# Two output projection tiles per layer as one seven-product block multiplication

## The chip, the core and the metric

The kernel runs on one core of a Trainium2 chip, in one launch. The metric is the device time of a run in microseconds; lower is better. The engines are TensorE (PE: matrix products; PEld: its weight loads), VectorE (DVE), ScalarE (ACT), GpSimd (POOL) and SyncE (SP), which issues most DMA transfers. Each engine takes its own queue in order; a wait at the head of a queue holds all that stands behind it.

## The reference

Two layers of a hybrid decoder on 512 tokens and 16 learned meta tokens in front, width 1024, all in fp32:

```python
for l in range(DEPTH):                       # DEPTH = 2
    h = rmsnorm(h_res, norm_gain[l])
    proj = h @ w_in[l]
    u_pool, z_pool, c_q, c_kv, k_rope, z_mla, g_pool, g_mla = jnp.split(proj, IN_SPLIT_POINTS, axis=-1)
    y_pool = (pool_mix(u_pool, pool_w_group[l], pool_scale[l]) * silu(z_pool)) @ pool_w_up[l]
    o_mla = mla(c_q, c_kv, k_rope, pos, ...)          # 8 heads, latent queries and keys, causal
    y_mla = (o_mla * silu(z_mla)) @ mla_w_up[l]
    merged = sigmoid(g_pool) * y_pool + sigmoid(g_mla) * y_mla
    h_res = h_res + merged @ w_out[l]                 # 1024 x 1024
return h_res[:, N_META:]
```

The change is in the last product, `merged @ w_out[l]`.

## The kernel before

**Layout.** Activations lie transposed: channels on the 128 partitions, tokens along the free axis, eight tiles of 128 channels for the width of 1024. Layer 0 works on all 528 tokens, as two segments of 264 (`FULL`); layer 1 needs only the 512 real tokens after its keys and does them as one segment of 512 (`XTOK`), but its last output tile as two of 256.

**Matrix products.** fp32 accuracy is made from three passes: each operand is split into a high part and a low part, and `mm3` issues high x high, high x low, low x high into the same PSUM bank (lines 181, 182, 183). One chunk of weights is 128 x 512 fp32 (256 KB), four blocks of 128 x 128. SyncE loads it (`raw`, L114), ScalarE copies the high part (`whi`, L176), VectorE subtracts to get the low part (`wlo`, L177). [...]

**The order.** `plan` lists the products in the order of the kernel (`register`), and the generator `stream` runs through the weight chunks of the whole plan, keeps several loaded ahead, and yields after every few matmuls. `go` is the rest of the layer: it pulls `stream` along with `upto(name)`, `fill_now(ns)` (go on for so many nanoseconds of modelled matmul time) and puts element-wise work between; `after(ns, fn)` calls a function after so much modelled time. The engines' final queues are then written by a list scheduler that works through the whole program with its own cost model, and may move an instruction of an engine ahead of others.

**The stages around the change.** The last products of a layer are `mu0` to `mu7` (up-projection of attention, 512 deep, one weight chunk each) and `o0` to `o7` (output projection, 1024 deep, two chunks each). What `ev_mu` does for each mu tile and segment: VectorE multiplies with the gate out of PSUM (L980), GpSimd adds the pooling branch `am[m]` (L982), and `split` makes the high part on ScalarE (L275) and the low part on VectorE (L276); the results `mg[0..7]` (`hh`, `hl`) are the operand of all o tiles. Each o tile is 8 blocks x 3 passes: 24 matmuls per segment. `ev_o` reads the residual (from `xT`, in layer 1 from `scr`), adds 0.5 times the product on VectorE (L996; the halved factor belongs to the sigmoid), stores to `scr` or, in layer 1, to the output `yT`, and in layer 0 has the next layer's sum of squares begun (`square_x`). After `o7` of layer 0 the kernel splits the next layer's input (`split_h`).

**Other places that the change touches.** In the query phase `qr0`, `qr1`, `qn0` to `qn3` run (weights `wqb`), with the statistics in `stat` after `qr1`; attention follows, where GpSimd multiplies at L743 and L832/L834. `tmp()` and `sqt()` hand out scratch tiles, `slot(tag)` tiles with names that are shared over the layer, `mmt()` and `sct()` PSUM banks.

Of the kernel before, what the change touches and what calls it, by code (L numbers as in the profile page):

```python
# [55 lines left out]
SPL = 240  # L56
RET = 12500.0
WARM = 8


def cut(v, bits):
# [10 lines left out]
def trunk(ctx, tc, xT, xrow, mrow, pos, win, wkr, wqb, wkb, wvb, wgr, wpu, wmu, wout, gains, const, yT):  # L72
# [89 lines left out]
    class Gemm:  # L162
        def __init__(self, name, src, width, evac=None, xs=None, segs=None, body=None):
            self.name, self.src, self.width, self.alloc = name, src, width, mmt
            self.evac, self.xs, self.segs, self.body = evac, xs, segs, body
            self.spare = False

    loads = [0]

    def wload(src, n, spare):  # L170
        raw = early.pop(0) if early else fetch(src, n, rawt(), sp)
        loads[0] += 1
        pool, th, tl, nb = (tp, "th", "tl", 2) if loads[0] <= 2 or spare else (wp, "whi", "wlo", 3)
        hi = pool.tile([P, W if pool is tp else 512], F32R, tag=th, name=nm("whi"), bufs=nb)
        lo = pool.tile([P, W if pool is tp else 512], F32R, tag=tl, name=nm("wlo"), bufs=nb)
        act.activation(hi[:, :n], raw[:, :n], AF.Copy)  # L176
        dve.tensor_sub(lo[:, :n], raw[:, :n], hi[:, :n].bitcast(F32))  # L177
        return hi, lo

    def mm3(out, wh, wl, xh, xl, start, stop):  # L180
        first = pe.matmul(out, wh, xh, start=start, stop=False)  # L181
# [8 lines left out]
    def stream():  # L190
        flat = [(g_, c) for g_ in plan for c in range(0, g_.width, 512)]
        names = [g_.name for g_, c in flat]
        for i in (1, names.index((0, "o0")) + 1):
            flat[i], flat[i + 1] = flat[i + 1], flat[i]

        def load(i):
            g_, c = flat[i]
            n = min(512, g_.width - c)
# [118 lines left out]
    class Layer:  # L317
        def __init__(self, l):
            self.l, self.last = l, l == DEPTH - 1
            self.XS = XTOK if self.last else FULL  # L320
            self.x0 = NM if self.last else 0
            self.xt = xt if l == 0 else [None] * 8
            self.hs, self.us, self.zps = hbuf, [None] * 4, [None] * 4
            self.cs, self.cqs, self.ys, self.am = [None] * 2, [None] * 6, [None] * 4, [None] * 8
            self.kn, self.qn, self.zms, self.ogs = [None] * 4, [None] * 4, [None] * 4, [None] * 4
            self.qr, self.qf = [None] * 2, [None] * 2
            self.gms, self.mg, self.xr, self.vw = [None] * 8, [None] * 8, [None] * 8, []
            self.made = [None] * 8
            self.csq, self.xsq = [None] * 2, [None] * 8
            self.sq = []  # L330
            self.hosted = self.st = self.acc = self.inv = self.cinv = self.kraw = self.kp = None

        def g(self, c):
            return gn[:, self.l * N_GAIN + c:self.l * N_GAIN + c + 1]
# [640 lines left out]
        def ev_mu(self, m):  # L975
            def ev(ps, a, b):
                if a == self.x0:
                    self.mg[m] = self.hs[m]
                t = tmp()
                dve.scalar_tensor_tensor(out=t[:, :b - a], in0=self.gms[m][:, a:b], scalar=1.0, in1=ps,  # L980
                                         op0=ALU.add, op1=ALU.mult)
                gp.tensor_add(t[:, :b - a], t[:, :b - a], self.am[m][:, a:b])  # L982
                split(*self.mg[m], t[:, :b - a], a, b)
            return ev

        def ev_o(self, m, nxt):
            def ev(ps, a, b):
# [19 lines left out]
        def register(self, nxt):  # L1007
            l, XS = self.l, self.XS
            wi = lambda t: win[l, t]
            hs, ys, cs = (lambda: self.hs), (lambda: self.ys), (lambda: self.cs)  # L1010

            def add(name, src, width, **kw):
                plan.append(Gemm((l, name), src, width, **kw))

            for m in range(2):
                if (l, m) == (0, 1):
                    plan[-1].alloc = sct
                add(f"ckv{m}", wi(MT_CKV + m), D, evac=self.ev_ckv(m), xs=hs, segs=FULL)
# [24 lines left out]
            y(2)  # L1043
            cq(5)
            y(3)
            for r in range(2):
                add(f"qr{r}", wqb[l, r], 768, evac=self.ev_qr(r), xs=lambda: self.cqs, segs=XS)
            for p in range(4):
                add(f"qn{p}", wqb[l, 2 + p], 768, evac=self.ev_qn(p), xs=lambda: self.cqs, segs=XS)
            for m in range(8):  # L1050
                add(f"pu{m}", wpu[l, m], 512, evac=self.ev_pu(m), xs=ys, segs=XS)
            for m in range(4):
                add(f"zm{m}", wi(MT_ZM + m), D, evac=self.ev_silu(self.zms, "u", m), xs=hs, segs=XS)
            for m in range(8):
                add(f"gp{m}", wi(MT_GP + m), D, evac=self.ev_gp(m), xs=hs, segs=XS)
            for m in range(8):
                add(f"gm{m}", wi(MT_GM + m), D, evac=self.ev_gm(m), xs=hs, segs=XS)
            for m in range(8):
                add(f"mu{m}", wmu[l, m], 512, evac=self.ev_mu(m), xs=lambda: self.ogs, segs=XS)
                plan[-1].spare = m % 2 == 1  # L1060
                if (l, m) in ((0, 2), (0, 5)):
                    plan[-1].alloc = sct
            mg = lambda: self.mg
            for m in range(8):
                add(f"o{m}", wout[l, m], D, evac=self.ev_o(m, nxt), xs=mg,
                    segs=[(NM, NM + SEQ // 2), (NM + SEQ // 2, T)] if self.last and m == 7 else XS)
                if (l, m) == (0, 1):
                    plan[-1].alloc = sct

        def gap(self):  # L1070
            fill(FILL[self.l], (self.l, RESERVE[self.l]))

        def go(self, nxt):
# [143 lines left out]
```

## Time and profile before

| | |
|---|---|
| median of 3 runs | 770.41 us (770.23 to 770.59) |
| profiled execution, span from first to last instruction | 768.5 us |
| PE busy | 763.8 us, 99% of the span |
| DVE busy | 544.1 us, 71% |
| ACT busy | 408.9 us, 53% |
| POOL busy | 201.6 us, 26% |
| HBM read, written | 76.69 MB, 4.29 MB |

The only time that the profile gives for its execution is the span; it leaves out what lies ahead of the first and behind the last instruction, and is 1.9 us below the median. Busy time is the time in which an engine had an instruction running; a row of the timeline has start and duration in us, the engine, the line of the kernel, and out<-in. A row's count x2 or x3 means neighbours of the same kind drawn together. "Idle ... <-" names what ended the idle time ahead of it. A row of the windows has, for each engine, busy time and in brackets the instructions, then the granted TensorE clock (1.00 is full speed), the share of the DMA engines and GB/s.

### The profile page before, as it was taken

To read this page: it belongs to the slowest core of one execution; us is meant where nothing else is said; L and a number is where in the kernel's file an instruction comes from. 1 tells how busy PE (TensorE), PEld (TensorE's weight loads), DVE (VectorE), ACT (ScalarE), POOL (GpSimd) and SP (SyncE) were. 2 spreads that over 40 slices of the span, in tenths; PEclk is the share of its full clock that TensorE was granted. 3 is DMA by queue.
4 is the path that set the end of the run, shared out by engine and by line. 5 is a ranking of instruction groups with operands and counts; after the bars stand their busy time and mean duration, and the time that the engine had idled before them with its cause. 6 is when DMAs were issued, how large, how long until landed. Compare 5 with 4: busy or idle time off the path is not lost.

```text
span 768.5 us, 14355 instructions
## 1 busy us (share of the span) xinstructions
PE 763.8 (99%) x5195; PEld 697.9 (91%) x5195; DVE 544.1 (71%) x1179; ACT 408.9 (53%) x892; POOL 201.6 (26%) x251
## 2 busy tenths in 40 slices
PE   9999999999999999999999999999999999999998
PEld 9999999999999999999997898887888888888887
DVE  5588687357899977785376486773677989775842
ACT  6755656545556665634264355454446666664320
POOL 2026204012242233052220262040132434420500
PEclk9999999999999999999999999999999999999999
DMA  8533233343223222325642333334433332222372
GB/s 293 160 113 98 75 97 98 104 141 105 89 79 91 84 71 70 107 71 169 178 133 97 110 86 89 96 87 127 125 119 90 94 93 77 82 69 70 119 222 98
DMA packets 54931, 84.05 MB, mean 109 GB/s; under 512 B 10006, under 2 KB 18582, under 8 KB 54860
## 3 DMA queue, kind: packets, MB, share of 16 engines
q1 hardware_dynamic: 54716, 82.87, 35.6%
q8 instruction: 41, 0.67, 0.4%
q14 instruction: 30, 0.25, 0.1%
q10 hardware_dynamic: 144, 0.26, 0.1%
HBM read 76.69 MB, written 4.29 MB: 105 GB/s over the span
## 4 chain that ended last, share of the span: by engine, by line
PE 99%; DMA 0%; ACT 0%; DVE 0%; SPq 0%; issue 0%; ACTq 0%
PE mm L181 29%; PE mm L183 29%; PE mm L182 29%; PE mm L859 2%; PE S L181 2%; PE S L182 2%; PE S L183 2%; PE o L876 1%; PE o L872 1%; PE S L503 1%; PE S L470 0%; DMA xb<-xT 0%; PE S L806 0%; PE mm L922 0%; PE mm L395 0%; PE S L872 0%
## 5 line engine op out<-in xcount | busy, mean ns | idle before, releaser
L181 PE MATMUL mm<-hh,whi 128*128 128x264 f32 (+2 forms) x1080 | 339.9, 317 | 0.0
L182 PE MATMUL mm<-hl,whi 128*128 128x264 f32 (+2 forms) x1080 | 338.2, 314 | 0.0
L183 PE MATMUL mm<-hh,wlo 128*128 128x264 f32 (+2 forms) x1080 | 337.1, 315 | 0.0
L177 DVE TENSOR_TENSOR wlo<-raw,whi 128x512 fp32r<-128x512 f32 (+2 forms) x251 | 186.7, 748 | 98.6 <-ACT whi L176 94.6
L176 ACT ACTIVATE whi<-raw 128x512 fp32r<-128x512 f32 (+2 forms) x251 | 150.2, 602 | 181.3 <-PE mm L182 135.3
L181 PEld LDWEIGHTS mm<-hh,whi 128*128 128x128 f32 x1080 | 202.5, 188 | 12.9 <-ACT kp L474 0.4
L182 PEld LDWEIGHTS mm<-hl,whi 128*128 128x128 f32 x1080 | 203.0, 188 | 12.2
L183 PEld LDWEIGHTS mm<-hh,wlo 128*128 128x128 f32 x1080 | 201.9, 188 | 12.2
L743 POOL TENSOR_TENSOR tmp<-kp,bc 64x528 f32<-64x528 f32 x16 | 25.6, 1600 | 123.9 <-PE mm L183 70.0
L604 POOL TENSOR_TENSOR racc<-racc,tmp 128x264 f32<-128x264 f32 (+1 forms) x15 | 14.3, 956 | 133.1 <-ACT tmp L603 133.1
L832 POOL TENSOR_TENSOR pm<-pa,rs 128x16 f32<-128x16 f32 x32 | 9.1, 285 | 126.1 <-DVE rs L827 126.1
L982 POOL TENSOR_TENSOR tmp<-tmp,xb 128x264 f32<-128x264 f32 (+1 forms) x24 | 26.9, 1138 | 56.0 <-DVE tmp L980 55.9
L774 DVE CUSTOM_DVE_ANT_0 S<-S,maskw,nqs 128x400 f32<-128x400 f32 (+4 forms) x80 | 38.4, 499 | 4.4 <-PE S L183 4.0
L781 ACT ACTIVATE cq<-S,bia 128x400 f32<-128x400 f32 (+2 forms) x48 | 24.6, 516 | 27.1 <-DVE bia L774 18.1
L181 PE MATMUL mm<-u,whi 128*128 128x264 f32 (+1 forms) x108 | 34.7, 322 | 0.0
L181 PE MATMUL mm<-cq,whi 128*128 128x264 f32 (+1 forms) x108 | 34.7, 321 | 0.0
L183 PE MATMUL mm<-u,wlo 128*128 128x264 f32 (+1 forms) x108 | 34.7, 321 | 0.0
L183 PE MATMUL mm<-cq,wlo 128*128 128x264 f32 (+1 forms) x108 | 34.5, 321 | 0.0
L182 PE MATMUL mm<-cq,whi 128*128 128x264 f32 (+1 forms) x108 | 34.5, 321 | 0.0
L834 POOL TENSOR_TENSOR cq<-cq,rs 128x384 f32<-128x384 f32 (+1 forms) x32 | 32.8, 1024 | 0.0
L276 DVE TENSOR_TENSOR tl<-mm,th 128x384 fp32r<-128x384 f32 (+1 forms) x48 | 27.9, 596 | 5.0 <-ACT th L275 4.8
L275 ACT ACTIVATE th<-mm 128x384 fp32r<-128x384 f32 (+1 forms) x48 | 24.1, 523 | 10.2 <-PE mm L859 9.2
(270 smaller groups left out, 1378.6 us busy)
## 6 DMA issues: line engine op xcount, KB each, us to landing
raw<-win SPq DMA_DIRECT2D x143, 256.0 KB, 2.6
raw<-wout SPq DMA_DIRECT2D x32, 256.0 KB, 3.0
bc<-kdr SPq DMA_DIRECT2D x16, 264.0 KB, 3.6
raw<-wpu SPq DMA_DIRECT2D x16, 256.0 KB, 2.7
raw<-wmu SPq DMA_DIRECT2D x16, 256.0 KB, 2.7
raw<-wqb SPq DMA_DIRECT2D x12, 256.0 KB, 2.6
xb<-xT SPq DMA_DIRECT2D x8, 264.0 KB, 5.7
tmp<-xT SPq DMA_DIRECT2D x16, 132.0 KB, 3.4
```

Of the source, the lines that this page charges most:

```text
L176: act.activation(hi[:, :n], raw[:, :n], AF.Copy)
L177: dve.tensor_sub(lo[:, :n], raw[:, :n], hi[:, :n].bitcast(F32))
L181: first = pe.matmul(out, wh, xh, start=start, stop=False)
L182: pe.matmul(out, wh, xl, start=False, stop=False)
L183: newest[0] = pe.matmul(out, wl, xh, start=False, stop=stop)
L275: act.activation(hi[:, a:b], src, AF.Copy)
L276: return dve.tensor_sub(lo[:, a:b], src, hi[:, a:b].bitcast(F32))
L743: gp.tensor_mul(kf[r0:r0 + 64, :], self.kp[r0:r0 + 64, :], bc[r0:r0 + 64, :])]
L774: return dve.tensor_tensor_reduce(out=sv, in0=sv, in1=mask, scale=nqs[:, i, h:h + 1], scalar=3e38, op0=ALU.add, op1=ALU.min, accum_out=bia ...
L781: act.activation(pv, sv, AF.Exp, scale=-1.0, bias=bia[:, i:i + 1], accum_out=rs[:, c:c + 1])
L834: gp.tensor_mul(pt[i][:, NM:], pt[i][:, NM:], rs[:, i:i + 1].to_broadcast([P, n - NM]))
L982: gp.tensor_add(t[:, :b - a], t[:, :b - a], self.am[m][:, a:b])
```

## The change

Tiles `o6` and `o7` of each layer become one block product. With the merged activations X (1024 deep: upper half 0 to 3, lower half 4 to 7; tokens in two halves) and the two 1024 x 128 weight tiles, the 2 x 2 block product is made from seven products of sums (Strassen's scheme in a variant with shared sums) instead of eight: per product 4 blocks x 3 passes = 12 matmuls of 264 columns (layer 0) or 256 (layer 1).

- `weight_sums`, called after the statistics that follow `qr1`: four sums of weight blocks, formed in DRAM. SyncE issues four copies from `wout` to new DRAM tiles, GpSimd four DMAs that add to them (`accum_op=ALU.add`), with `fill_now(2 * LAG)` between. `pair_operand` gives `stream` the seven chunks: three plain, four sums. All seven are split into high and low as before; that is seven chunks instead of four.
- `combine`: sums of activation quarters on VectorE, 16 per layer; `combine_split`: their high part on ScalarE (L1023 of the new kernel) and low part on VectorE (L1024), 16 each per layer. The first sums start from `ev_mu` with a lag, the others and the splits between `up("mu7")` and `up("o7")` with `fill_now(PACE)` ahead of each.
- `ev_mu`: the pooling sum is written into `am[m]` in place (the sums need it in fp32), and the split reads it there.
- `pair_body`: the seven products use three PSUM banks; a bank is added up over several products (`start=False`), and VectorE adds the bank with 0.5 or -0.5 to the residual after each (L1069), seven times instead of four (layer 0) or three (layer 1). The residual is loaded as one whole tile per m. The built queue has the products of layer 1 in the order 0, 1, 3, 2, 5, 4, 6.

The core of the diff:

```diff
+PAIRS = (3,)
+PACE = 1000.0
...
             def ev(ps, a, b):
...
-                gp.tensor_add(t[:, :b - a], t[:, :b - a], self.am[m][:, a:b])
-                split(*self.mg[m], t[:, :b - a], a, b)
+                f = self.am[m][:, a:b]
+                gp.tensor_add(f, t[:, :b - a], f)
+                split(*self.mg[m], f, a, b)
+                if b == T:
+                    after(LAG, lambda: self.combine(1 if m < 4 else 3, m % 4))
...
+        def combine(self, w, k):
...
+            if w == 1:
+                eng.tensor_sub(f, lo[:, a0:b0], lo[:, a1:b1])
+            elif w == 2:
+                eng.tensor_add(f, hi[:, a1:b1], self.tf[1, k])
+            elif w == 3:
+                eng.tensor_sub(f, hi[:, a1:b1], lo[:, a1:b1])
+            else:
+                eng.tensor_sub(f, self.tf[2, k], hi[:, a0:b0])
+
+        def combine_split(self, w, k):
+            if w in (2, 4):
+                self.combine(w, k)
...
+            act.activation(th, f, AF.Copy, scale=sign)
+            dve.scalar_tensor_tensor(out=tl, in0=f, scalar=sign, in1=th.bitcast(F32), op0=ALU.mult, op1=ALU.subtract)
+
+        def weight_sums(self):
+            acc = lambda d, src: behind(gp.dma_start(d, src, accum_op=ALU.add, max_dma_last_dim=2048), newest[0])
...
+                for d, src in ((s1, w(1, 0)), (s3, w(1, 0)), (s2, w(0, 0)), (s4, w(0, 1))):
+                    behind(sp.dma_start(d, src), newest[0])
+                fill_now(2 * LAG)
+                acc(s1, w(1, 1))
+                acc(s3, w(0, 0))
+                fill_now(2 * LAG)
+                acc(s2, s1)
+                fill_now(2 * LAG)
+                acc(s4, s2)
+
+        def pair_operand(self, p):
...
+                return wload((raw(0, 0), raw(0, 1), s2, s1, s3, s4, raw(1, 1))[i], 512, i % 2 == 1)
...
+            def product(ps, w, xs, start):
+                for k in range(4):
+                    wh, wl = (x[:, k * P:(k + 1) * P] for x in w)
+                    xh, xl = xs[k]
+                    for j, (u, v) in enumerate(((wh, xh), (wh, xl), (wl, xh))):
+                        newest[0] = pe.matmul(ps, u, v, start=start and k == 0 and j == 0, stop=k == 3 and j == 2,
+                                              skip_group_check=not start)
...
+                if i == 0:
+                    product(B, w, quarter(0, a0, b0), True)
+                    add(m1, a0, b0, B, 0.5, False)
+                elif i == 1:
+                    product(A, w, quarter(4, a0, b0), True)
+                    add(m1, a0, b0, A, 0.5, True)
+                elif i == 2:
+                    product(B, w, ts(2), False)
+                    add(m1, a1, b1, B, 0.5, False)
+                elif i == 3:
+                    product(C, w, ts(1), True)
+                    add(m2, a1, b1, C, -0.5, False)
+                elif i == 4:
+                    product(B, w, ts(3), False)
+                    add(m2, a1, b1, B, -0.5, True)
+                elif i == 5:
+                    product(C, w, quarter(4, a1, b1), False)
+                    add(m1, a1, b1, C, 0.5, True)
+                else:
+                    product(B, w, ts(4), False)
+                    add(m2, a0, b0, B, -0.5, True)
+                    done.add((self.l, f"o{m2}"))
+                yield 12 * (n / 2.4)
...
-            for m in range(8):
-                add(f"o{m}", wout[l, m], D, evac=self.ev_o(m, nxt), xs=mg,
-                    segs=[(NM, NM + SEQ // 2), (NM + SEQ // 2, T)] if self.last and m == 7 else XS)
+            for m in range(2 * PAIRS[0]):
+                add(f"o{m}", wout[l, m], D, evac=self.ev_o(m, nxt), xs=mg, segs=XS)
...
+            for p in PAIRS:
+                add(f"o{2 * p + 1}", None, 7 * 512, body=self.pair_body(p, nxt))
+                plan[-1].operand = self.pair_operand(p)
...
+            self.weight_sums()
             up("qn3")
...
+            up("mu7")
+            flush()
+            for w in (2, 1, 3, 4):
+                for k in range(4):
+                    fill_now(PACE)
+                    self.combine_split(w, k)
             up("o7")
```

More of the change, by code (lines that the diff above doesn't have):

```diff
@@ L165, in __init__, with parts @@
             self.evac, self.xs, self.segs, self.body = evac, xs, segs, body
-            self.spare = False
+            self.spare, self.operand = False, None
     loads = [0]
+    def parts(raw, n, spare, eng):
+        pool, th, tl, nb = (tp, "th", "tl", 2) if spare else (wp, "whi", "wlo", 3)
+        hi = pool.tile([P, W if pool is tp else 512], F32R, tag=th, name=nm("whi"), bufs=nb)
+        lo = pool.tile([P, W if pool is tp else 512], F32R, tag=tl, name=nm("wlo"), bufs=nb)
+        act.activation(hi[:, :n], raw[:, :n], AF.Copy)
+        eng.tensor_sub(lo[:, :n], raw[:, :n], hi[:, :n].bitcast(F32))
+        return hi, lo
     def wload(src, n, spare):
@@ L172, in wload @@
         loads[0] += 1
[L173 to L178, printed above, removed]
+        return parts(raw, n, loads[0] <= 2 or spare, dve)
     def mm3(out, wh, wl, xh, xl, start, stop):
@@ new lines, in pair_operand, with operand, pair_body, quarter @@
+        def pair_operand(self, p):
+            def operand(i):
+                raw = lambda odd, c: wout[self.l, 2 * p + odd, :, 512 * c:512 * c + 512]
+                s1, s2, s3, s4 = self.ws[p]
+                return wload((raw(0, 0), raw(0, 1), s2, s1, s3, s4, raw(1, 1))[i], 512, i % 2 == 1)
+            return operand
+        def pair_body(self, p, nxt):
+            st = {}
+            (a0, b0), (a1, b1) = self.HV
+            n = b0 - a0
+            m1, m2 = 2 * p, 2 * p + 1
+            def quarter(k0, a, b):
+                return [tuple(x[:, a:b] for x in self.mg[k]) for k in range(k0, k0 + 4)]
+            def product(ps, w, xs, start):
[5 more added lines that the diff above has]
+                                              skip_group_check=not start)
+            def add(m, a, b, ps, scale, last):
+                xr = st["x", m]
+                out = xb[:, m] if last and not self.last else xr
+                dve.scalar_tensor_tensor(out=out[:, a:b], in0=ps, scalar=scale, in1=xr[:, a:b], op0=ALU.mult, op1=ALU.add)
+                if not last:
+                    return
+                c = max(a, NM)
+                if self.last:
+                    sp.dma_start(yT[:, m, c - NM:b - NM], out[:, c:b])
+                    return
+                sp.dma_start(scr[:, m, c - NM:b - NM], out[:, c:b])
+                st["n", m] = st.get(("n", m), 0) + 1
+                if st["n", m] == 2:
+                    nxt.xt[m] = out
+                    nxt.square_x(m)
+            def body(i, w):
+                if i == 0:
+                    for m in (m1, m2):
+                        st["x", m] = tmp()
+                        src = scr[:, m, :] if self.last else xT[:, m, :]
+                        sp.dma_start(st["x", m][:, self.x0:T], src)
+                    st["b"], st["a"], st["c"] = mmt()[:, :n], sct()[:, :n], mmt()[:, :n]
+                ts = lambda w_: [self.ts[w_, k] for k in range(4)]
+                A, B, C = st["a"], st["b"], st["c"]
+                if i == 0:
+                    product(B, w, quarter(0, a0, b0), True)
[20 more added lines that the diff above has]
+                yield 12 * (n / 2.4)
+            return body
```

19 lines of the change are left out of this document (added).

## The prediction

> **What bounds the kernel now.** I read the page from the top: the span, the share of each engine, the granted clock, then the chain that ended last.
>
> ```profile
> span 768.5 us, 14355 instructions
> ...
> PE 763.8 (99%) x5195; PEld 697.9 (91%) x5195; DVE 544.1 (71%) x1179; ACT 408.9 (53%) x892; POOL 201.6 (26%) x251
> ...
> PEclk9999999999999999999999999999999999999999
> ...
> PE 99%; DMA 0%; ACT 0%; DVE 0%; SPq 0%; issue 0%; ACTq 0%
> ```
>
> TensorE is busy for 99% of the span at the full clock, and the chain is TensorE from end to end. So a removed matmul is a gain at its own spacing, and anything that makes TensorE wait is a loss of the whole wait. The 768.5 us are this one execution; the median of the runs is 770.41, 1.9 us more, and I carry those 1.9 unchanged.
>
> A whole-kernel share of 71% for VectorE says nothing about the stages that the change touches, so I next read the windows. The first and third are the merge stages (mu0 to mu7) of layer 0 and layer 1, the second and fourth begin where o0 to o7 start.
>
> ```profile
> core 0: us, PE busy (x) PEld busy (x) DVE busy (x) ACT busy (x) POOL busy (x), PEclk, DMA share, GB/s
> 329.40:351.60 22.20, 22.20 (x184) 22.20 (x184) 20.71 (x38) 10.51 (x23) 14.58 (x16) 1.00 0.27 78
> 351.60:390.00 38.40, 38.40 (x318) 38.40 (x317) 16.11 (x30) 13.16 (x23) 5.32 (x4) 1.00 0.66 193
> 708.00:729.20 21.20, 21.20 (x94) 17.16 (x93) 19.97 (x24) 9.63 (x16) 12.29 (x8) 1.00 0.32 95
> 729.20:768.00 38.80, 35.89 (x179) 30.00 (x177) 12.75 (x20) 6.95 (x11) 0.00 (x0) 1.00 0.52 165
> ```
>
> In the merge stages VectorE is busy 20.71 of 22.20 us and 19.97 of 21.20: full, while TensorE still runs without a gap. In the output stages it is busy 16.11 of 38.40 and 12.75 of 38.80. Where the added VectorE work lands in its queue therefore decides.
>
> **What is removed.** Spacings come from the TensorE timeline, from the starts of two matmuls with the same shape:
>
> ```profile
> 353.27 0.28 PE L183 MATMUL mm<-hh,wlo 128*128 128x264 f32 x1
> ...
> 358.27 0.29 PE L182 MATMUL mm<-hl,whi 128*128 128x264 f32 x1
> ...
> 731.05 0.39 PE L182 MATMUL mm<-hl,whi 128*128 128x512 f32 x1
> ...
> 735.21 0.39 PE L182 MATMUL mm<-hl,whi 128*128 128x512 f32 x1
> ...
> 762.09 0.28 PE L181 MATMUL mm<-hh,whi 128*128 128x256 f32 x1
> ...
> 764.57 0.28 PE L181 MATMUL mm<-hh,whi 128*128 128x256 f32 x1
> ```
>
> There are 41, 18 and 21 spacings between the members of each couple: 0.122, 0.231 and 0.118 us. Layer 0 goes from 96 matmuls of 264 columns to 84: 12 x 0.122 = 1.46 us saved. Layer 1 had 24 of 512 for o6 and 48 of 256 for o7, and gets 84 of 256: 24 x 0.231 + 48 x 0.118 - 84 x 0.118 = 1.29 us. Together 2.75 us, all on the path.
>
> **What is added on VectorE, and where.** Each layer gets 16 half-width sums and differences and 16 second halves of a split, on 264 or 256 columns, with 16 ScalarE copies between. The program spaces the second sort by 1 us of TensorE work, but the built VectorE queue decides, and there I count. VectorE takes its queue in order, so every operation of a combine behind the last merge eviction delays what is queued after it: the splits of mu6 and mu7 that o0 reads, and the low halves (wlo) of the weight tiles of o1 and o2.
>
> The price of one operation and the state of the stage before:
>
> ```profile
> L276 DVE TENSOR_TENSOR hl<-tmp,hh 128x264 fp32r<-128x264 f32 x16 | 11.3, 720 | 1.2 <-ACT hh L275 1.2
> ...
> L982 POOL TENSOR_TENSOR tmp<-tmp,xb 128x264 f32<-128x264 f32 x16 | 14.6, 927 | 27.8 <-DVE tmp L980 27.6
> ...
> 329.42 1.11 DVE L980 SCALAR_TENSOR_TENSOR tmp<-cq,mm 128x264 f32<-128x264 f32 x3 [2.98 <-PE mm L183]
> ...
> 348.94 0.42 DVE L276 TENSOR_TENSOR hl<-tmp,hh 128x264 fp32r<-128x264 f32 x1
> 349.29 0.42 DVE L980 SCALAR_TENSOR_TENSOR tmp<-cq,mm 128x264 f32<-128x264 f32 x1
> ...
> 351.20 0.43 DVE L276 TENSOR_TENSOR hl<-tmp,hh 128x264 fp32r<-128x264 f32 x1 [0.20 <-ACT hh L275]
> ...
> L276 DVE TENSOR_TENSOR hl<-tmp,hh 128x512 fp32r<-128x512 f32 x8 | 7.1, 905 | 1.1 <-ACT hh L275 1.1
> ...
> 708.07 1.28 DVE L980 SCALAR_TENSOR_TENSOR tmp<-cq,mm 128x512 f32<-128x512 f32 x2 [2.86 <-PE mm L183]
> ...
> 720.50 1.28 DVE L276 TENSOR_TENSOR hl<-tmp,hh 128x512 fp32r<-128x512 f32 x2
> ...
> 727.87 0.68 DVE L276 TENSOR_TENSOR hl<-tmp,hh 128x512 fp32r<-128x512 f32 x1
> ```
>
> Undisturbed and back to back, 264 columns cost 0.34 us ((1.11 - 0.43) / 2, and 349.29 - 348.94 for the subtraction of two SBUF operands) and 512 columns 0.60 (1.28 - 0.68). The stage of before takes more: from 329.42 to the end of the last split at 351.63 it lasted 22.2 us for 32 operations of 264 and 6 of 512, which at those spacings are 14.5. Idle time is 1.2, so 6.5 us are the price of running beside the GpSimd additions of line 982: the subtractions of line 276 took 0.72 on average instead of 0.42. In layer 1, from 708.07 to 728.55, 23 operations of 512 are 13.8 of 20.5 us, idle is 1.1, so that price is 5.6.
>
> [...]
>
> *Layer 0.* In the new queue 68 operations stand from the first merge eviction up to and including the low half of o2's first weight tile: 8 of 512 and 60 of 264, 28 of these new. That is 8 x 0.60 + 60 x 0.34 = 25.2 us; I add the 6.5 of before, since the same 16 GpSimd additions run: ready at 329.42 + 31.7 = 361.1. TensorE meets that tile's low half at its 2883rd matmul, which is the row at 358.27 (both orders have as many before it). Wait: 361.1 - 358.3 = 2.8 us. Part of it comes earlier (the second split of mu7 stands at place 57, ready by the same sum near 357 and wanted at 354.7), but these are one backlog, not added twice. The idle 1.2 us of before is used up in this.
>
> *Layer 1.* 56 operations up to the low half of o2's second tile: 27 of 512 and 29 of 256 (priced as 264): 16.2 + 9.9 = 26.1, with 5.6 gives 739.8. TensorE wants it where before had the row at 735.21 (12 matmuls fewer had gone before in layer 0). Wait: 4.6 us. Again most is there earlier: the split of mu7 (42 operations, ready at 733.9) is wanted at 731.05.
>
> After that VectorE is less than half busy and catches up; its seven evictions in place of three or four per pair, and three more wlo, are hidden by this. Bounds: nothing subtracts from the backlog except contention that goes away with longer stretches without GpSimd. If a quarter of it did, the waits are 1.2 and 3.2. Above, the new operations that stand before the last merge eviction (11 in layer 0, 9 in layer 1) may pay as line 276 does: 11 x 0.30 + 9 x 0.22 = 5.3 more. I take the middle value, 7.4, because GpSimd's busy 14.58 us is what can be collided with, and its number of additions is the same.
>
> **The pair's own order.** In layer 1 product 6 adds up in the same PSUM bank as product 4, which stands directly before it, and must wait for VectorE to have read it out. Layer 1's last evictions of before:
>
> ```profile
> 763.39 0.28 PE L183 MATMUL mm<-hh,wlo 128*128 128x256 f32 x1
> ...
> 763.71 0.42 DVE L996 SCALAR_TENSOR_TENSOR tmp<-mm,tmp 128x256 f32<-128x256 f32 x1 [3.57 <-PE mm L183]
> ...
> 765.13 0.42 DVE L996 SCALAR_TENSOR_TENSOR tmp<-mm,tmp 128x256 f32<-128x256 f32 x1 [0.99 <-PE mm L183]
> ```
>
> From the start of the last matmul of a half to the end of its eviction are 763.71 + 0.42 - 763.39 = 0.74 us; less the 0.12 that the next matmul would have waited anyway, and some 0.1 for the signal back, 0.7 us. In layer 0 next-layer matmuls stand between the two products, so nothing. All other products have another product of 1.4 us or more between. The end (one eviction of 256, one store) is as before.
>
> **The weight sums** go past two queues.
>
> ```profile
> 166.74 1.80 POOL L743 TENSOR_TENSOR tmp<-kp,bc 64x528 f32<-64x528 f32 x1 [35.06 <-PE mm L183]
> ...
> 552.27 2.41 POOL L743 TENSOR_TENSOR tmp<-kp,bc 64x528 f32<-64x528 f32 x1 [34.97 <-PE mm L183]
> ...
> raw<-wqb SPq DMA_DIRECT2D x12, 256.0 KB, 2.6
> ...
> raw<-wout SPq DMA_DIRECT2D x32, 256.0 KB, 3.0
> ```
>
> GpSimd issues four accumulating transfers per layer, each waiting for an earlier one; behind them in its queue stands line 743, after an idle 35 us, so they are hidden if the four take under 35 / 4 = 8.7 us each. SyncE issues four DRAM copies of 256 KB ahead of the next query weight tiles. No row shows a copy between two DRAM places; the nearest is 2.6 us for a load of that size. Four side by side up to four in a row give 2.6 to 10.4 us, against about 10 us by which those tiles are requested early: 0 to 1 us of wait each layer. I take 0. Six more tiles of 256 KB in the two output stages: one per product of 1.46 us is 180 GB/s, beside 193 in the window above, hidden.
>
> [...]
>
> **Sum.** Span 768.5 - 2.75 + 2.8 + 4.6 + 0.7 = 773.9, and with the 1.9 around it 775.8 us: the arithmetic saved is less than what TensorE waits for VectorE. By the bounds, 1.2 + 3.2 and 5.3 more, with 0 to 2 for the copies: 772.7 to 783.
>
> **Rivals.**
>
> *The combines are covered (faster).* If contention beside GpSimd is no fixed price, but the queue's added operations fill time in which VectorE would have waited anyway, the ready times without any contention are 329.42 + 25.2 = 354.6 and 708.07 + 26.1 = 734.2, both ahead of the need (358.3 and 735.2). Then only the 0.7 is lost: 768.5 + 1.9 - 2.75 + 0.7 = 768.4. For it: the ends of VectorE's waits are that close. Against it: 6.5 and 5.6 us are measured in this stage, and it decides only if over half of the one and nearly all of the other vanish. 0.2.
>
> *One layer waits, the other hardly.* Layer 1 has the larger backlog; with layer 0 covered the sum is 770.4 - 2.75 + 4.6 + 0.7 = 773.0; with layer 1 covered 771.2; with half of each gone 772.1, and close to no change if more. 0.15, of which 0.05 falls within 0.2% of before.
>
> *The transfers bite (slower).* Accumulations that take over 8.7 us each keep GpSimd from line 743: at 11 us each by 44 - 35 = 9 us in each layer, 18 in all, less what attention has in store. Or the copies hold up the query weights: 3 us in each layer are 6, so 782 and more. For it: no row shows either. Against it: the 35 us of idle time. 0.1.
>
> *It doesn't do what it says.* If the pair runs with as many matmuls, nothing is saved: the built queue has 84 per layer. Under 0.01.
>
> **How the numbers follow.** The forecast has 0.55, at 775.8, its own range 772.7 to 780. About 0.2% (1.5 us) is what a measurement of this kernel can tell from no change. Faster is the covered case, 0.2; within 0.2% 0.06; the rest, 0.74, slower. The range must reach into the covered case below and stop short of the transfers above: 768.2 to 781.
>
> **What would show it.** In the profile after: TensorE idle for about 3 us between 354 and 362 and some 4.5 us near 730 to 740, released by VectorE's lines of the split and of wlo; VectorE without a gap from the first merge eviction to there; one idle of 0.7 us before the last product; 84 matmuls in each pair at 0.122 and 0.118 us. I'm wrong if TensorE has no such gap (then VectorE's operations cost less than their rows beside GpSimd), or if its idle time lies in the query stage or at line 743.

## The result and the profile after

The changed kernel takes 787.89 us (median of 4 runs, 786.77 to 790.25), the kernel before beside it 770.50 us: a ratio of 1.023, 95% interval 1.0212 to 1.0248. It is slower by 17.4 us; the forecast was 775.8 us, with 781.0 as its upper end. The sign and the first mechanism were right, the size was not.

The page of the changed kernel, at the places where the page of before was shown:

```profile
span 785.0 us, 14496 instructions
...
PE 765.4 (98%) x5195; PEld 696.5 (89%) x5195; DVE 573.1 (73%) x1256; ACT 423.0 (54%) x930; POOL 206.3 (26%) x259
...
PE 87%; DVE 8%; DMA 3%; issue 1%; ACT 1%; POOL 0%; SPq 0%; DVEq 0%; ACTq 0%
```

The chain, TensorE for 99% before, now runs through VectorE for 8% of 785.0 us and through DMA for 3%: some 63 and 24 us of the path that ended last. That is not what TensorE lost, since it worked beside much of it; its loss is read from its own waits. Its timeline marks each idle time and what ended it. The merge and output stage of layer 0, then of layer 1 up to o2:

```profile
349.25 0.39 PE L186 MATMUL mm<-hh,whi 128*128 128x264 f32 x1 [1.93 <-DVE tmp L990]
...
356.08 0.39 PE L187 MATMUL mm<-hl,whi 128*128 128x264 f32 x1 [0.35 <-DVE hl L283]
...
358.48 0.39 PE L187 MATMUL mm<-hl,whi 128*128 128x264 f32 x1 [0.55 <-DVE hl L283]
...
362.79 0.39 PE L188 MATMUL mm<-hh,wlo 128*128 128x264 f32 x1 [0.49 <-DVE wlo L177]
...
737.39 0.50 PE L188 MATMUL mm<-hh,wlo 128*128 128x512 f32 x1 [1.40 <-DVE wlo L177]
...
747.64 0.50 PE L188 MATMUL mm<-hh,wlo 128*128 128x512 f32 x1 [1.32 <-DVE wlo L177]
```

Every one is released by VectorE: a merge eviction (L990), the low half of a split (L283), the low half of a chunk (L177). The last row of layer 0 is the wait for o2's first chunk, the last of layer 1 that for o2's second, as predicted. The largest wait of layer 0, 1.93 us at 349.25, comes before the stretch that the prediction named (354 to 362): there the merge evictions themselves were late, as early sums and splits stood among them in VectorE's queue. VectorE's own windows, from the first merge eviction to the end of those low halves:

```profile
329.64:362.73 33.09, 29.82 (x238) 28.97 (x236) 33.09 (x69) 18.10 (x42) 14.63 (x16) 1.00 0.22 69
714.72:747.58 32.86, 28.75 (x118) 21.31 (x116) 32.86 (x57) 16.46 (x35) 12.19 (x8) 1.00 0.29 91
```

In both, the third pair of numbers (VectorE) is busy for the whole stretch, 33.09 of 33.09 and 32.86 of 32.86.

The second half of the loss is inside the pairs, where 0.7 us had been expected:

```profile
391.32 0.48 PE L1063 MATMUL mm<-kh,whi 128*128 128x264 f32 x2 [0.97 <-ACT hh L350]
...
394.69 0.36 PE L1063 MATMUL mm<-hh,whi 128*128 128x264 f32 x1 [1.67 <-DVE tmp L1069]
...
770.98 0.47 PE L1063 MATMUL mm<-kh,whi 128*128 128x256 f32 x2 [0.33 <-DVE tmp L1069]
776.25 0.36 PE L1063 MATMUL mm<-hh,whi 128*128 128x256 f32 x1 [3.62 <-DVE tmp L1069]
```

For a balance I add up, in each profile, how much the spacing between two matmul starts goes over the spacing of that shape (by 0.095 us or more; this also takes in first matmuls after a wait: behind each of the 16 waits of 0.2 us or more in the changed kernel the next matmul came 0.07 to 0.11 us later than its shape's spacing). "Merge" is the stretch up to o2 or so, "pair" the rest of the output stage with the boundary to the next layer:

| TensorE's lost time, us | merge, layer 0 | pair, layer 0 | merge, layer 1 | pair, layer 1 |
|---|---|---|---|---|
| before | 0.0 | 0.0 | 0.0 | 0.0 |
| changed | 4.4 | 3.4 | 5.8 | 5.1 |
| no combines | 0.0 | 1.4 | 0.0 | 1.7 |
| own residual tile | 4.4 | 3.5 | 5.9 | 1.7 |
| no weight sums | 4.2 | 3.0 | 5.9 | 6.0 |
| combines after o1 | 0.0 | 3.9 | 0.0 | 2.1 |
| next splits after the pair | 4.4 | 3.3 | 5.8 | 7.2 |
| combines late, kept right | 0.0 | 2.7 | 1.7 | 1.7 |
| evictions before splits | 0.0 | 3.7 | 1.7 | 4.2 |
| pair in the last layer only | 0.0 | 0.0 | 1.6 | 2.8 |
| early chunks | 3.6 | 0.4 | 6.3 | 0.8 |
| no combines, early chunks | 0.0 | 0.6 | 1.0 | 0.0 |
| all mended | 0.5 | 0.7 | 1.0 | 0.0 |
| mended, splits later | 0.0 | 0.9 | 0.0 | 0.0 |

Where a wait was followed by a stretch at half the clock (0.50 in the windows of the last section), the slow matmuls are in the sums, with 1.3 to 2.2 us each: in layer 1's pairs in the 7.2, 6.0 and 4.2 us, in layer 0's pair in the 3.7 us of "evictions before splits", in the merge stages in the 4.2 us of "no weight sums" and the 3.6 and 6.3 us of "early chunks".

The changed kernel loses 18.7 us and saves 2.75, net 16.0, against 16.5 in the spans (785.0 - 768.5); some 0.2 of the rest lies ahead of the merge stage of layer 0 (first eviction at 329.64, before at 329.42).

### The profile page after: what moved, and what is told of

Its sections match the earlier page's. It is cut to its first block, busy times and chain, and to the rows that moved or that the text cites. A ratio compares the mean times of both kernels' runs of the same rounds, so it can differ in the third digit from the quotient of the medians.

```text
span 785.0 us, 14496 instructions
## 1 busy us (share of the span) xinstructions
PE 765.4 (98%) x5195; PEld 696.5 (89%) x5195; DVE 573.1 (73%) x1256; ACT 423.0 (54%) x930; POOL 206.3 (26%) x259
## 4 chain that ended last, share of the span: by engine, by line
PE 87%; DVE 8%; DMA 3%; issue 1%; ACT 1%; POOL 0%; SPq 0%; DVEq 0%; ACTq 0%
PE mm L186 25%; PE mm L188 25%; PE mm L187 24%; PE mm L869 2%; DVE wlo L177 2%; PE S L186 2%; DMA raw<-wout 2%; PE S L187 2%; PE S L188 2%; DVE hl L283 1%; PE mm L1063 1%; DVE tmp L990 1%; PE o L886 1%; PE o L882 1%; PE S L513 1%
## 5 line engine op out<-in xcount | busy, mean ns | idle before, releaser
L186 PE MATMUL mm<-hh,whi 128*128 128x264 f32 (+1 forms) x1024 | 323.3, 318 | 2.1 <-DVE tmp L990 2.1
L187 PE MATMUL mm<-hl,whi 128*128 128x264 f32 (+1 forms) x1024 | 322.2, 316 | 2.1 <-DVE hl L283 2.1
L188 PE MATMUL mm<-hh,wlo 128*128 128x264 f32 (+1 forms) x1024 | 319.7, 316 | 3.2 <-DVE wlo L177 3.2
L177 DVE TENSOR_TENSOR wlo<-raw,whi 128x512 fp32r<-128x512 f32 (+2 forms) x257 | 190.6, 745 | 107.5 <-ACT whi L176 103.9
L176 ACT ACTIVATE whi<-raw 128x512 fp32r<-128x512 f32 (+2 forms) x257 | 153.3, 602 | 176.5 <-PE mm L187 93.2
L187 PEld LDWEIGHTS mm<-hl,whi 128*128 128x128 f32 x1024 | 192.6, 188 | 15.8 <-DVE hl L283 4.2
L186 PEld LDWEIGHTS mm<-hh,whi 128*128 128x128 f32 x1024 | 192.3, 188 | 15.1 <-DVE tmp L990 2.8
L188 PEld LDWEIGHTS mm<-hh,wlo 128*128 128x128 f32 x1024 | 191.1, 188 | 16.0 <-DVE wlo L177 4.3
L993 POOL TENSOR_TENSOR xb<-tmp,xb 128x264 f32<-128x264 f32 (+1 forms) x24 | 26.8, 1134 | 63.2 <-DVE tmp L990 63.2
L283 DVE TENSOR_TENSOR tl<-mm,th 128x384 fp32r<-128x384 f32 (+1 forms) x48 | 27.9, 595 | 5.0 <-ACT th L282 4.8
```

The source lines that it names most:

```text
L177: eng.tensor_sub(lo[:, :n], raw[:, :n], hi[:, :n].bitcast(F32))
L187: pe.matmul(out, wh, xl, start=False, stop=False)
L188: newest[0] = pe.matmul(out, wl, xh, start=False, stop=stop)
L283: return dve.tensor_sub(lo[:, a:b], src, hi[:, a:b].bitcast(F32))
L993: gp.tensor_add(f, t[:, :b - a], f)
```

## The experiments

**No combines.** `combine` and `combine_split` are not called:

```diff
-                ts = lambda w_: [self.ts[w_, k] for k in range(4)]
+                ts = lambda w_: [tuple(x[:, a0:b0] for x in self.ogs[k]) for k in range(4)]
```

> Left out: the sums of activation quarters and their splits (16 + 16 on VectorE, 16 on ScalarE per layer); the products of sums read the operand of the mu tiles instead, so the same 84 matmuls per pair run. Theory A (the waits before o2 are VectorE's backlog of combines; the waits inside the pair are something else): TensorE's 4.3 us of waits before o2 in layer 0 and 5.8 us in layer 1 vanish, the 3.5 and 5.0 us inside the pairs stay: 787.9 - 10.1 = about 778 us. Rival B (the pairs' waits are the same backlog, passed on through late loads): they vanish too, about 769.5 us.

Measured: 771.95 us, ratio 1.0024 (1.0011 to 1.0037). The waits of the merge stages are gone entirely, so they were the backlog of combines. But the pairs' waits shrink too, from 8.5 to 3.1 us: it lies between theory A (778) and B (769.5), nearer to B. What waits inside the pairs was partly the backlog handed on, partly its own.

**Own residual tile.**

```diff
-                        st["x", m] = tmp()
+                        st["x", m] = slot(f"q{m - 2}") if self.last else tmp()
```

> In layer 1 the pair's two residual tiles get tiles of their own instead of two of the three scratch tiles, so that their load no longer waits for an earlier output store to land. Theory A (that wait, at the head of SyncE's queue, held the chunk loads behind it, and TensorE then waited 3.8 us in the middle of layer 1's pair): about 784 us, with that wait gone or under 1 us. Rival (three raw buffers and 4 us to landing are too slow for a chunk per 1.42 us, whatever SyncE waits for): 3.8 us stay nearly whole, 787 to 788 us.

Measured: 786.32 us (the profiled run 784.02), ratio 1.0202 (1.0185 to 1.0219). In the medians this is 1.6 us, and the intervals of both kernels overlap, so the time alone shows little. The two profiled executions, both at a clock of 1.000, are 2.7 us apart, and in the new profile the wait of 3.62 us is gone: layer 1's pair went from 5.1 to 1.7 us of lost time. SyncE's timeline of the changed kernel, its waits from 760 to 770, and then ScalarE's and VectorE's rows show what had held it:

```profile
764.23 0.34 SPq L1131 DMA_DIRECT2D yT<-tmp  x1
764.83 0.32 SPq L116 DMA_DIRECT2D raw<-ws  x1
768.09 0.32 SPq L1087 DMA_DIRECT2D tmp<-scr  x1
768.73 0.32 SPq L116 DMA_DIRECT2D raw<-ws  x1
769.33 0.33 SPq L116 DMA_DIRECT2D raw<-wout  x1
...
SPq L1087 <- DMA yT<-tmp: 6.1, 2, 3.2
...
773.48 1.15 ACT L176 ACTIVATE whi<-raw 128x512 fp32r<-128x512 f32 x2 [4.18 <-DMA raw<-wout]
...
774.15 0.69 DVE L177 TENSOR_TENSOR wlo<-raw,whi 128x512 fp32r<-128x512 f32 x1 [3.31 <-ACT whi L176]
```

Between 765.2 and 768.1 SyncE issues nothing: the residual load (L1087) waits for the scratch tile of an output store that has not landed (6.1 us in two waits, the longer 3.2), and two chunk loads stand behind it. They are issued at 768.73 and 769.33 and land some 4 us later. ScalarE stands idle until 773.48, VectorE until 774.15, and the matmul at 776.25 gets its bank only after the low halves and evictions that follow.

**No weight sums.** Left out are the DMAs of `weight_sums`; `pair_operand` loads plain blocks.

> Left out: the copies and accumulating DMAs that form the sums of weight blocks; the pair loads plain blocks of the same size instead. Theory A (they lie beside other work, as in the prediction): within 1 us of 787.9. Rival C (they slow the query phase, or sums in DRAM load more slowly than weights): 2 us or more faster, 786 or less.

Measured: 787.41 us, ratio 1.0211 (1.0192 to 1.0229), against 1.0230 with them. The sums in DRAM lie beside other work, as predicted.

**Combines after o1.**

```diff
-                if b == T:
-                    after(LAG, lambda: self.combine(1 if m < 4 else 3, m % 4))
...
+            up("o1")
+            for w in (1, 2, 3, 4):
                 for k in range(4):
                     fill_now(PACE)
+                    self.combine(w, k)
                     self.combine_split(w, k)
```

with `follow(made, newest[0])` on each sum, so that the scheduler does not put it earlier. In layer 0 the sums here read tiles that `o0` and its followers have already overwritten with the new residual: only the time counts.

> All combines and their splits of both layers are queued after the last matmul of o1, one per microsecond of matmul time, instead of from the mu stage on. Theory A: VectorE has the time between o2 and o5 (it is under half busy there), the waits before o2 vanish and the pair's waits stay: about 778 us. Rival D (the 32 operations cost as much wherever they stand, since they delay the chunks' low halves in the output stage): 784 to 788 us.

Measured: 773.72 us, ratio 1.0040 (1.0024 to 1.0056), 14 us below the changed kernel with the same instructions. The merge stages are at 0.0 lost; rival D is out. The gain is 4 us more than theory A gave. 3.0 us of it are in layer 1's pair, which went from 5.1 to 2.1 us without anything in it being changed, so there the backlog had been handed on (a load into a raw buffer is issued only when a low half has freed it: in the changed kernel SyncE's chunk loads from 740 us on waited 4.1 us for low halves). Layer 0's pair did not gain: it loses 3.9 us, against 3.4 in the changed kernel and 1.4 without combines. So in layer 0 the combines cost some 2 us inside the pair wherever they stand, as long as the feed of chunks is as built.

**Next splits after the pair.**

```diff
                 made = act.activation(hh[:, a:b], x[:, a:b], AF.Copy, scale=gk)
+                if self.l:
+                    follow(made, newest[0])
```

> The changed kernel with one thing moved: the splits of the next layer's input (ScalarE and VectorE, 528 columns, some 0.7 us each), which stand between the pair's evictions in layer 0, are queued after the pair's last matmul. Theory A (in layer 0 the pair's 3.5 us of waits are evictions that stand behind these splits in VectorE's queue): inside the pair about 1 us is left (0.7 of it because nothing now stands between products 4 and 6), and 1.5 to 2 us come up at the next layer's first product, which must wait for the splits; total 786 to 788. Rival E (the evictions wait for the low halves of weight chunks whose slots are not free yet): the pair's waits stay at 3 us or more and the total is 789 or more.

Measured: 790.27 us, ratio 1.0251 (1.0234 to 1.0268). 3.3 us are still lost at layer 0's pair. Some 0.8 of them are new, as product 6 now follows product 4 directly, so 2.5 of the 3.4 us remain: theory A falls, rival E holds in the main. The longer time proves nothing beyond that: all runs had a mean clock of 0.996, and the changed kernel's runs at 0.996 took 788.85 and 790.25 us. The evictions were late because a low half stood ahead of them that was itself late; the ninth run shows which late thing it was.

**Combines late, kept right.** The sums whose sources `o0` and `o1` overwrite stay at the end of the mu stage, the others come after `o1`; own residual tile; each product of layer 1 follows the one before it.

> The combines for blocks 0 and 1 that read tiles which o0 and o1 overwrite stay near the end of the mu stage (4 to 6 operations), all others come after o1; layer 1's pair has residual tiles of its own, and its products are held in the order 0 to 6, so that products 4 and 6 no longer adjoin. Theory A (only the place of the combines and the load held up in SyncE's queue cost): no waits before o2, layer 1's pair under 1 us, layer 0's pair about 3.5 us as in the run with late combines: 770.5 - 2.75 + 4 = about 772. Rival D (what is deferred delays the chunks of o3 to o5): 775 or more.

Measured: 777.00 us, ratio 1.0082 (1.0067 to 1.0097), 5 us above the expectation. Four sums that I left in layer 1's mu stage (their splits stand after `o1`) go with 1.7 us lost there, which layer 1 didn't need (its residual does not go over those tiles), and both pairs still lose 4.4. Another 1.7 us were lost before the merge stage of layer 0 (first eviction at 331.13, before at 329.42).

**Evictions before splits.** In layer 0, `follow(low, adds[...])` puts the first four evictions ahead of the next layer's splits.

> As the run before (combines late), and in layer 0 each of the pair's first four evictions is queued ahead of the next layer's split that stood ahead of it. Theory A: layer 0's pair loses 1 to 2 us of its 3.5 us of waits, about 770.5 us. Rival E: no change against the run before.

Measured: 776.60 us, ratio 1.0077 (1.0054 to 1.0099), within the spread of the run before. Layer 0's pair shows 3.7 us, of which some 1.4 are matmuls at half the clock (granted 0.94 on average from 385 to 412); the rest, 2.4, is little less than the 2.7 of the run before: rival E again.

**Pair in the last layer only.**

> As the run with late combines, but only layer 1 has the pair; layer 0 keeps its eight plain output tiles. Theory A: the 1.29 us saved in layer 1 stay but for some tenths, so 769.3 to 770.0, just below the kernel before. Rival: the chunk every 1.42 us cannot be loaded and split in time even so, and 1 us or more is lost in the pair: 770.5 or above.

Measured: 775.19 us, ratio 1.0056 (1.0041 to 1.0071). The rival holds, and not even one pair pays like this: 1.6 us at the left-over early sums and 2.8 inside the pair, against 1.29 saved.

**Early chunks.** Back to the changed kernel, with only this:

```diff
-                return wload((raw(0, 0), raw(0, 1), s2, s1, s3, s4, raw(1, 1))[i], 512, i % 2 == 1)
+                src = (raw(0, 0), raw(0, 1), s2, s1, s3, s4, raw(1, 1))[i]
+                return parts(fetch(src, 512, slot(f"cq{i // 2}") if i % 2 else rawt(), sp), 512, i % 2 == 1, dve)
```

> The changed kernel with one thing added: the second, fourth and sixth weight chunk of each pair are loaded into tiles of their own that lie free in this stage, so that their loads stand in SyncE's queue ahead of the merge stage's evictions instead of behind stores and residual loads. Theory A (inside the pairs TensorE waits for the feed of chunks: load, high part, low part, each through one of three raw buffers at 1.42 us per chunk): of the 8.5 us of waits inside the pairs some 4 go, the 10.1 before o2 stay: 783 to 784 us. Rival E (the feed is set by VectorE's queue, not by the loads): 786 or more.

Measured: 779.85 us, ratio 1.0111 (1.0097 to 1.0124): 8 us gained, twice what was expected, although two stretches at half the clock cost some 3 us in its profile (last section). The pairs lose 1.2 us in place of 8.5. So the feed of chunks was the pairs' cause; three of seven chunks that need no raw buffer of the ring are enough. The run does not tell the wait for a buffer from the place in SyncE's queue, since a tile of its own changes both.

**No combines, early chunks.** As the first run (combines left out), with the three chunks early, the own residual tile and layer 1's products in order.

> As the run without combines (they are left out; the products of sums read the operand of the mu tiles), with the three chunks of each pair loaded early, layer 1's residual in tiles of its own and its products in the order 0 to 6. Theory A: with backlog and feed taken away the saving of the arithmetic shows: 770.5 - 2.75 + at most 1 = 767.8 to 769. Rival (product pace: a chunk each 1.42 us cannot be split by ScalarE and VectorE in time): 770.5 or more.

Measured: 769.88 us, ratio 0.9986 (0.9977 to 0.9996). That is above theory A's 767.8 to 769 and below the rival's 770.5. With 1.6 us still lost, 770.84 - 2.75 + 1.6 = 769.7: within some tenths, the saved matmuls are worth what their spacings said.

**All mended.** The same with the combines in, placed as in the sixth run but in layer 1 all after `o1`.

> The whole computation: combines after o1 (in layer 0 those for blocks 0 and 1 near the end of the mu stage, in layer 1 none there), three chunks of each pair loaded early, layer 1's residual in tiles of its own, its products in order. Theory A: no waits before o2, 1 to 3 us inside layer 0's pair, under 1 in layer 1's: 769 to 771.5 us. Rival D (the deferred combines delay the low halves of later chunks): 773 or more.

Measured: 770.61 us, ratio 0.9993 (0.9983 to 1.0003): 17 us below the changed kernel, level with the kernel before, and within theory A's 769 to 771.5, though 1.5 us are still lost before o2, where it had none. Of what is left, 0.9 us is the split of mu7 in layer 1, behind low halves of the early chunks that VectorE now took in the mu stage.

**Mended, splits later.** `follow(made, mark)` on the high parts of the pair's chunks, with `mark` the last matmul at the end of `o1`.

> The whole computation, as the mended run before, and the high and low parts of the early chunks are queued after the mu stage's splits instead of between them (they stood ahead of the split of mu6 and mu7 in layer 1, where TensorE waited 0.86 us). Theory A (VectorE's queue in the mu stage has no room even for two operations of 512): that wait goes, 770.6 - 0.9 = 769.5 to 769.9, just below the kernel before. Rival: the time goes into another wait, 770.3 or above.

Measured: 769.28 us against 770.48, ratio 0.9989 (0.9980 to 0.9998). The merge stages are at 0.0 in both layers. It leaves nothing out and is the one such version whose interval lies below the kernel before: by 1.2 us of the 2.75, with 0.2 to 1.5 in the interval. Of the rest, 0.9 us are lost in layer 0's pair, and layer 0's merge stage begins 1.6 us later than before (330.98 against 329.42).

## Why the prediction was wrong

*What is removed: right.* 2.75 us were worked out; the run without combines and with early chunks bears this out within some tenths.

*The backlog of VectorE: the mechanism right, its size too small.* The forecast had 2.8 and 4.6 us, the profile 4.4 and 5.8. The count of operations and their undisturbed price held; the term that was mis-sized is the price of running beside GpSimd, which I left at the 6.5 and 5.6 us of before. It measures 33.1 - 25.2 = 7.9 and 32.9 - 26.1 = 6.8 us. VectorE's groups in layer 0's window of the changed kernel:

```profile
L283 DVE TENSOR_TENSOR hl<-xb,hh 128x264 fp32r<-128x264 f32 x16 | 8.9, 568 | 0.0
...
L1006 DVE TENSOR_TENSOR sq<-xb 128x264 f32<-128x264 f32 x4 | 3.4, 847 | 0.0
L1010 DVE TENSOR_TENSOR sq<-xb 128x264 f32<-128x264 f32 x4 | 2.8, 698 | 0.0
L1024 DVE SCALAR_TENSOR_TENSOR u<-sq,u 128x264 fp32r<-128x264 f32 x4 | 2.2, 562 | 0.0
...
L1008 DVE TENSOR_TENSOR sq<-xb,sq 128x264 f32<-128x264 f32 x4 | 1.5, 421 | 0.0
```

The early sums took 847 and 698 ns on average (mixtures of 0.42 and about 0.98 us), the late ones, behind GpSimd's last addition, 421; the splits of line 283 paid less than before (568, before 720). In both layers and both kernels, every VectorE operation of these windows that took longer than its undisturbed time overlapped a GpSimd addition; those that overlapped none took their undisturbed time. Counted by durations, the excess is 5.5 and 5.3 us before, 7.6 and 6.8 in the changed kernel, and of the latter 3.9 and 3.4 fall on new operations. So the collisions moved over to the new operations, and the price grew by 1.4 and 1.2 us over what the sum had (7.9 against 6.5, 6.8 against 5.6), less than the upper bound of 3.3 that the prediction had for layer 0. The prediction kept the price because GpSimd's additions are the same in number; the longer queue of VectorE nevertheless lost more beside them. The merge evictions of line 990, which read one input from PSUM, kept their 0.41 to 0.43 us in layer 0's window of the changed kernel, also the 6 of 16 that had more than 0.1 us of a GpSimd addition beside them. (The row that the prediction calls TensorE's 2883rd matmul, at 358.27, is the 2936th in the trace, in both kernels; the row is the right one.)

*"After that VectorE is less than half busy and catches up": the step that failed.* This had the pairs lose nothing but the 0.7 us of their order; they lost 8.5. VectorE did catch up on the plain tiles (busy 11.1 of 22 us from 363 to 385, 7.75 of 17 from 748 to 765), but the loads did not. The output stage is a ring: SyncE issues a chunk's load when a low half frees one of three raw buffers, the low half stands in VectorE's queue behind evictions, and those wait for residuals that SyncE loads between the chunks. That such a ring, once late, stays late as long as nothing in it is faster than TensorE is my estimate, from the trip worked out below. The run with early chunks shows that the feed was the cause (1.2 us lost), the run with the residual's own tile which load held up layer 1. Which link of the ring holds layer 0's pair is argued, not shown.

*"One per product of 1.46 us is 180 GB/s, hidden": wrong measure.* By the windows bandwidth was not at its limit: in the pairs' stretches (second and third row) less was moved than in the stretch before, where TensorE was busy throughout:

```profile
363.00:375.00 12.00, 12.00 (x100) 12.00 (x100) 6.85 (x17) 4.47 (x7) 1.33 (x1) 1.00 0.82 242
385.00:400.00 15.00, 12.15 (x95) 11.57 (x95) 11.95 (x21) 9.65 (x16) 1.37 (x1) 1.00 0.70 209
765.00:777.00 12.00, 8.06 (x61) 7.44 (x60) 5.12 (x10) 2.93 (x5) 0.00 (x0) 1.00 0.47 162
```

The trip is what fits. A chunk's load takes 3.4 us to land in the changed kernel, its high part 0.6, its low part 0.6 to 0.7, and SyncE issues the next load for the buffer between 0.03 us (at 753.08) and 2.8 us (at 762.05) later. That is an estimate of about 5 us for three buffers, 1.7 us per chunk, where a product takes 1.42 to 1.46; the shortest trip from issue to issue between 740 and 770 us, 747.61 to 753.08, took 5.5. With o tiles, two chunks in 5.5 to 5.9 us, this had never shown. The run with early chunks took 7.3 us off the pairs, the run with the residual's own tile 3.4. The two are not to be added: with early chunks SyncE's residual loads still wait 6.0 us for the output stores, and layer 1's pair loses only 0.8. The forecast was too low by 12.1 us: 7.8 are the pairs (8.5 instead of 0.7), 2.8 the backlog (10.2 instead of 7.4), and 1.1 lie between the profiled run and the median.

*Product 6 behind product 4: right where the order was as built.* 0.7 us were expected in layer 1; the timeline's spacings give 0.68 over the normal one at 779.84. The signal back, 0.1 us in the sum, took 0.06: the eviction ended at 779.78.

*The weight sums: right.* The accumulating transfers:

```profile
ws<-wout SPq DMA_DIRECT2D x4, 256.0 KB, 3.8
...
ws<-wout POOLq DMA_DIRECT2D x2, 256.0 KB, 6.9
ws<-ws POOLq DMA_DIRECT2D x2, 256.0 KB, 4.3
```

6.9 and 4.3 us to landing are under the 8.7 that would have been one too many; leaving them out moves nothing.

*Rivals.* "The transfers bite" gave a time near the measured one by another mechanism, which the third run rules out. The ready time without contention ("the combines are covered") did not come about in the changed kernel: both layers waited.

What stays open: the runs with late combines reach layer 0's merge stage 0.3 to 1.7 us later than the kernel before (up to 1.0 of it in the query phase), the changed kernel only 0.2; why the combines cost layer 0's pair some 2 us even where they stand late; and whether the last 0.9 us at the boundary of the mended kernel can go.

## What to carry to other kernels

Before work is added to an engine that is half idle over the whole kernel, read the window in which it will stand: here VectorE had 1.2 us free in 22, and the same 64 operations cost 10 us there and, placed after `o1` with three chunks of each pair loaded early, nothing that can be told (1.6 us of waits in the merge stages and pairs without them, 0.9 in the last run with them). When a product becomes shorter, compare the trip of its operand (issue, landing, conversions, buffer back) divided by the number of buffers with its new length (here 1.7 us by the estimate above, and 1.42 to 1.46), not the bandwidth. And a load that waits in an in-order queue delays all loads behind it, so a tile of its own for a residual (3.4 us of waits here) can be worth more than saved matmuls (2.75 us).

## What the runs showed of the hardware

TensorE's clock was not among the costs that I had counted, and in some profiles it added to long waits. In the run with early chunks, one wait of 2.9 us in layer 1 was followed by this:

```profile
732.51 0.39 PE L186 MATMUL mm<-hh,whi 128*128 128x512 f32 x1
732.74 0.28 PE L1064 MATMUL S<-hh,whi 128*128 128x256 f32 x1
735.94 0.80 PE L188 MATMUL mm<-hh,wlo 128*128 128x512 f32 x1 [2.93 <-DVE wlo L177]
736.54 0.63 PE L186 MATMUL mm<-hh,whi 128*128 128x512 f32 x1
736.96 0.63 PE L187 MATMUL mm<-hl,whi 128*128 128x512 f32 x1
...
739.09 0.39 PE L186 MATMUL mm<-hh,whi 128*128 128x512 f32 x1
```

and the windows of that run give the granted clock around it:

```profile
725.00:735.00 10.00, 6.90 (x30) 1.00 0.39 124
735.00:740.00 5.00, 4.06 (x13) 0.66 0.36 105
740.00:748.00 8.00, 8.00 (x39) 1.00 0.37 118
```

For about 3 us the spacing of 512 columns is 0.42 us instead of 0.23, then it is normal again; some 1.4 us are lost on top of the wait. A shorter wait was enough as well: the first row below is in layer 0 of the same run, with the windows behind the two waits (clock 0.50 in both), and the last window is the changed kernel's behind its wait of 1.93 us at 349.25:

```profile
349.78 0.46 PE L186 MATMUL mm<-hh,whi 128*128 128x264 f32 x1 [1.80 <-DVE tmp L990]
...
350.00:353.40 3.40, 3.40 (x17) 0.50 0.29 87
736.00:739.10 3.10, 3.10 (x8) 0.50 0.48 158
...
349.30:352.50 3.20, 3.20 (x26) 1.00 0.22 69
```

The changed kernel's longest wait, 3.62 us at 776.25, has a clock of 1.00 behind it too. Over the fourteen profiles, TensorE has 19 waits of 1.5 us or more behind the first 20 us; seven of them, of 1.58 to 3.50 us, were followed by half the clock, and twelve, of 1.52 to 3.62 us, were not. So the length of a single wait does not decide it. The spread of the changed kernel's runs goes with this: their mean clocks are 1.000, 0.998, 0.996 and 0.996 at 786.77, 786.93, 788.85 and 790.25 us, and the median lies 1.1 us above the profiled run.
